# Vector work of the mixers moved from VectorE to GpSimd in a two-layer hybrid decoder

## The chip, the cores and the metric

The kernel runs on one core of one Trainium2 chip. The metric is device time in microseconds, the median of several runs. PE is TensorE, DVE VectorE, ACT ScalarE, Pool (POOL) GpSimd, and SP SyncE, which here issues nearly all DMAs. Each engine takes its instructions in the order of the program, and waits at the head of its queue where an instruction's inputs are not there yet.

## What is computed

Two layers over 1024 tokens of width 1024, all in float32. A layer is, from the reference:

```python
h = rms_norm(x, g_pre_mix)
z = h @ w_in
...
mix = jnp.concatenate([out_m, out_s.astype(x.dtype), out_d], axis=-1) @ w_out
x = x + rms_norm(mix, g_post_mix)
h2 = rms_norm(x, g_pre_mlp)
u = jnp.square(jax.nn.relu(h2 @ w_up))
x = x + rms_norm(u @ w_down, g_post_mlp)
```

The three mixers share the projection z: an mLSTM in chunks of 128 tokens (4 heads of 64), a causal sliding-window attention (window 128, 8 query heads on 2 key heads, sinks in the denominator), and a differential attention (4 heads, each with two maps of width 32, the second subtracted with a factor lambda). The queries and keys of the two attentions are rotated (rope): of the halves x1 and x2 of a head, x1 cos - x2 sin and x2 cos + x1 sin.

## The kernel before

**High and low parts.** Matmul operands are kept as a high part, rounded to the reduced float format that PE takes at full speed, and a low part, the rest. A product is three matmuls (high by high, high by low, low by high) into one PSUM bank. The helper `split` (L90) makes the parts: ACT casts the source into the high part (L91), DVE subtracts it from the source (L92). `load_split` (L94) does this for rows of the mixers' output (L98, L99), and `load_w` (L101) for weights: SP loads a piece of 512 columns into one of the two staging tiles of the pool "raw" (L107), then `split` follows. With a gain (the MLP's up weights) L114 and L115 take its place.

**Stages of a layer.** Normalised, transposed rows hT and lT (high and low) are multiplied by w_in in three ways. `proj_tiles` (L254) keeps weights stationary and gives columns of z transposed: queries and keys of the differential attention (`p_d`), those of the window attention (`p_s`), the mLSTM's (`p_m`). `g2` makes gates and values, `nat_group` the mLSTM's values and output gates. For the attentions the evacuation rotates: `rope_pair` (L301) has the first halves of the heads in one PSUM tile and the second halves in another. It makes four products from PSUM (L309, L310, L311, L313) and one difference and one sum in SBUF (L312, L314), and `hi_lo` (L293) then makes the high part (ACT, L296), stores it to a scratch matrix in DRAM, makes the low part (DVE, L298) and stores that.

The differential attention loads keys and queries back (L450 to L463) and goes in stages over steps of one head and 256 queries: scores on PE (L491), a masked minimum on DVE (L494), the exponential on ACT (L497), the subtraction of the second map on DVE (L504), transposes on PE (L518), their split (L91, L92) and the product with the values (L526). `diff3` normalises: ACT squares, DVE makes the mean, Pool takes the power -1/2 (L151) and multiplies (L543), DVE scales (L545). The window attention (`swa1`, `swa2`) has the same parts over steps of 128 queries and one key head (L601 to L639); it divides the exponentials by the denominator before the transposes, the first head of four on ACT (L618), the others on DVE (L620). The mLSTM goes over 8 chunks (`mlstm1` to `mlstm3`). All three store to the scratch matrix mix_d.

The out-projection (`out_group`, L811) takes mix_d in two groups of four k tiles. For each of 8 token tiles it loads mixed rows ("mxl", L97), makes their parts (L98 on ACT, L99 on DVE), multiplies them by w_out (L833) and copies or adds the result (L839, L841). The second group ends each token tile with `post_mix`: norm, residual (L977, L979) and the transposed input of the MLP.

**What sets the order.** The code is traced once. A scheduler then orders the instructions of every engine by priority, the place in the trace, by what their inputs allow and by its own estimate of how long things take. `ahead(n)` gives the priority of n instructions earlier: 1000 for weight loads and evacuations, 100000 for mixed rows and accumulations. `run` interleaves the streams of the mixers. A tile that is allotted again waits for the last reader of the buffer it replaces ("e" has 4 buffers, which mixed rows share with the attention's exponentials; "raw" has 2; "ev" has 6). So a change of one instruction's engine can move others, on all engines.

Of the kernel before, what the change touches and what calls it, by code (L numbers as in the profile page):

```python
# [10 lines left out]
F32 = mybir.dt.float32  # L11
# [3 lines left out]
ALU = mybir.AluOpType  # L15
# [13 lines left out]
# columns of the packed per-layer vector that every partition gets  # L29
# [5 lines left out]
def hybrid_kernel(ctx: ExitStack, tc: tile.TileContext, x_in, w_t, w_g, w_v, w_out, w_up, w_down,  # L35
# [15 lines left out]
    pool("big", 6)      # 16 KB  # L51
    pool("whl", 2)      # 8 KB: stationary weight tiles, high | low
    pool("wd", 4)       # 4 KB: operands of the differential attention, moving weights
    pool("ws", 4)       # 4 KB: operands of the window attention, moving weights
    pool("e", 4)        # 4 KB
    pool("at", 2)       # 4 KB
    pool("pt", 2)       # 4 KB
    pool("ev", 6)       # 2 KB
    pool("raw", 2)      # 2 KB
    pool("od", 3)       # 1 KB  # L60
    pool("ys", 1)       # 2 KB
# [24 lines left out]
    def ahead(n):  # L86
        """trace with the priority of n instructions earlier"""
        return tc.high_priority(offset=n) if n else nullcontext()

    def split(hi, lo, src):  # L90
        nc.scalar.copy(hi, src)  # L91
        nc.vector.tensor_sub(lo, src, hi.bitcast(F32))  # L92

    def load_split(hi, lo, src):  # L94
        """high and low parts of a matrix in DRAM; the low part's place takes the raw values first"""
# [3 lines left out]
        nc.vector.tensor_sub(lo, raw, hi.bitcast(F32))  # L99

    def load_w(hi, lo, src, step, gain=None):  # L101
        """high and low parts of a weight tile, through a staging tile, step columns at a time;
        gain has a factor for every P columns"""
        for c in range(0, hi.shape[1], step):
# [3 lines left out]
            with ahead(1000):  # L108
                if gain is None:
                    split(hi[:, c:c + step], lo[:, c:c + step], r)  # L110
                    continue
# [15 lines left out]
    # ---- constants  # L127
# [5 lines left out]
    tri_u = mk[:, P:2 * P]          # 1 where row <= col  # L133
    sel_l = mk[:, 2 * P:3 * P]      # row 127 all ones
    jj = mk[:, 3 * P:4 * P]         # [I64 0; I64 0]
    m_st = mk[:, 4 * P:5 * P]       # 0 where row <= col, else NEG
    # for negated scores: zeros | current block, previous block | current block
# [22 lines left out]
    def pre_norm_transpose(src, g, h, hT, lT, t):  # L160
        """h = rmsnorm(src) * g (without g: a factor of the weights that follow), transposed and split into hT/lT[:, t, kt, :]"""
# [1025 lines left out]
```

## Time and profile before

| | us |
|---|---|
| median of 3 runs | 2562.7 |
| lowest and highest run | 2557.64 and 2574.75 |
| span of the profiled execution | 2570.0 |
| mixers of layer 0 (from the start to the MLP's first full stretch) | 0 to 602 |
| MLP of layer 0, with PE full | 602 to 1250 |
| mixers of layer 1 | 1250 to 1872 |
| MLP of layer 1 | 1872 to 2570 |

The profile page has the time of the profiled execution only as its span, from the first to the last instruction on the core. Lines of the profile give the line of the kernel, the engine and the operation, the written tile and the read ones, the shape and the count, then busy time in us and the mean of one in ns, then the idle time of the engine before these instructions and what ended it. A row of waits reads: the waiting engine and line, what it waited for, us in total, times, the longest. In the timeline a row has start and duration in us, and in brackets the idle time before it. The chain of waits is followed back from the last instruction through what released each step. "SPq" is SP's queue of DMA issues. The granted clock of PE was 0.973 of full speed over the span.

### The profile page before, as it was taken

To read this page: it belongs to the slowest core of one execution; us is meant where nothing else is said; L and a number is where in the kernel's file an instruction comes from. 1 tells how busy PE (TensorE), PEld (TensorE's weight loads), DVE (VectorE), ACT (ScalarE), POOL (GpSimd) and SP (SyncE) were. 2 spreads that over 40 slices of the span, in tenths; PEclk is the share of its full clock that TensorE was granted. 3 is DMA by queue.
4 is the path that set the end of the run, shared out by engine and by line. 5 is a ranking of instruction groups with operands and counts; after the bars stand their busy time and mean duration, and the time that the engine had idled before them with its cause. 6 is when DMAs were issued, how large, how long until landed. Compare 5 with 4: busy or idle time off the path is not lost.

```text
span 2570.0 us, 32598 instructions
## 1 busy us (share of the span) xinstructions
PE 2395.5 (93%) x11556; PEld 1994.0 (78%) x11556; DVE 1449.0 (56%) x3540; ACT 1072.3 (42%) x2625; POOL 96.4 (4%) x174
## 2 busy tenths in 40 slices
PE   8988988789999999999999988887999999999998
PEld 7767866667888888888778867766788888888887
DVE  5676867676144334433684976876842344334436
ACT  4244766655323222321433745765653123213312
POOL 0000010011000000000010000100100000000000
PEclk9998989899999999999999998998999999999999
DMA  4444336353012111211543334554521122012104
GB/s 168 146 139 131 94 97 162 104 156 116 26 58 66 40 34 58 66 32 34 170 149 105 106 128 130 149 129 112 165 87 34 37 61 66 28 39 66 61 24 161
DMA packets 172115, 240.02 MB, mean 93 GB/s; under 512 B 24048, under 2 KB 86704, under 8 KB 171952
## 3 DMA queue, kind: packets, MB, share of 16 engines
q1 hardware_dynamic: 169792, 234.29, 29.9%
q10 hardware_dynamic: 2160, 3.65, 0.4%
q8 instruction: 91, 1.49, 0.3%
q14 instruction: 72, 0.59, 0.1%
HBM read 185.38 MB, written 52.49 MB: 93 GB/s over the span
## 4 chain that ended last, share of the span: by engine, by line
PE 72%; DMA 12%; DVE 7%; ACT 4%; issue 2%; POOL 1%; SPq 1%; POOLq 0%; DVEq 0%; ACTq 0%
PE pu L997 26%; PE pd L1042 25%; PE pt L283 7%; DMA mxl<-mix_d 3%; DMA qs<-d_rope 2%; PE pn L354 2%; PE pg L354 2%; PE po L833 2%; POOL rs L151 1%; PE sp L491 1%; PE pv L526 1%; DMA rw<-in_w_t_dram 1%; PE trd L518 1%; PE ss L601 1%; DMA mix_d<-ys 1%
## 5 line engine op out<-in xcount | busy, mean ns | idle before, releaser
L997 PE MATMUL pu<-h2T,wu 128*128 128x512 f32 x3072 | 700.3, 389 | 0.0
L997 PEld LDWEIGHTS pu<-h2T,wu 128*128 128x128 f32 x3072 | 576.3, 188 | 119.4
L1042 PE MATMUL pd<-wdh,u 128*128 128x512 f32 x2048 | 634.2, 389 | 1.3 <-DVE acm L1053 1.3
L1042 PEld LDWEIGHTS pd<-wdh,u 128*128 128x128 f32 x2048 | 384.2, 188 | 81.2 <-DVE acm L1053 1.8
L1042 PE MATMUL pd<-wdl,u 128*128 128x512 f32 x1024 | 398.6, 389 | 0.0
L1053 DVE TENSOR_TENSOR acm<-acm,pd 128x512 f32<-128x512 f32 x224 | 152.4, 686 | 303.1 <-PE pd L1042 303.1
L1000 ACT ACTIVATE r<-pu 128x512 f32<-128x512 f32 x128 | 75.3, 588 | 537.6 <-PE pu L997 537.4
L283 PE MATMUL pt<-hT,wt 128*128 128x512 f32 x832 | 287.8, 411 | 2.3 <-DVE lamp L226 1.5
L114 ACT ACTIVATE wu<-rw,gk 128x128 fp32r<-128x128 f32 x512 | 160.6, 390 | 186.7 <-PE pu L997 129.1
L115 DVE SCALAR_TENSOR_TENSOR wu<-rw,gk,wu 128x128 fp32r<-128x128 f32 x512 | 154.9, 351 | 131.9 <-ACT wu L114 131.2
L1042 PEld LDWEIGHTS pd<-wdl,u 128*128 128x128 f32 x1024 | 192.2, 188 | 39.8
L1003 DVE TENSOR_TENSOR r<-r 128x512 f32<-128x512 f32 x128 | 88.4, 691 | 226.2 <-ACT u L1002 226.2
L283 PEld LDWEIGHTS pt<-hT,wt 128*128 128x128 f32 x832 | 160.5, 196 | 33.4 <-issue 2.1
L151 POOL TENSOR_TENSOR rs<-ms,mhalf 128x1 f32<-128x1 f32 (+2 forms) x112 | 84.5, 758 | 2355.8 <-DVE ms L149 2287.2
L283 PE MATMUL pt<-lT,wt 128*128 128x512 f32 x416 | 170.5, 410 | 0.0
L92 DVE TENSOR_TENSOR wdl<-rw,wdh 128x512 fp32r<-128x512 f32 x128 | 88.6, 692 | 104.8 <-ACT wdh L91 104.8
L833 PE MATMUL po<-woh,mxl 128*128 128x512 f32 x384 | 133.9, 410 | 0.0
L91 ACT CAST wdh<-rw 128x512 fp32r<-128x512 f32 x128 | 79.3, 619 | 129.2 <-DMA rw<-in_w_down_dram 129.1
L497 ACT ACTIVATE e<-e,nb 128x256 f32<-128x256 f32 (+7 forms) x128 | 99.3, 777 | 50.9 <-DVE nb L494 47.0
L491 PE MATMUL sp<-ks,qs 96*128 96x512 f32 (+2 forms) x192 | 74.2, 397 | 40.3 <-DMA qs<-d_rope 27.6
L354 PE MATMUL pn<-wv,hT 128*128 128x256 f32 x512 | 110.6, 298 | 0.2 <-ACT mv L694 0.2
L283 PEld LDWEIGHTS pt<-lT,wt 128*128 128x128 f32 x416 | 82.1, 197 | 14.6 <-issue 0.4
(221 smaller groups left out, 3339.6 us busy)
## 6 DMA issues: line engine op xcount, KB each, us to landing
rw<-in_w_up_dram SPq DMA_DIRECT2D x128, 256.0 KB
rw<-in_w_down_dram SPq DMA_DIRECT2D x128, 256.0 KB
rw<-in_w_t_dram SPq DMA_DIRECT2D x52, 256.0 KB
tab<-in_rope_dram SPq DMA_DIRECT2D x20, 512.0 KB
xt<-in_x_dram SPq DMA_DIRECT2D x16, 512.0 KB
d_rope<-rot SPq DMA_DIRECT2D x32, 256.0 KB
s_ropeq<-rot SPq DMA_DIRECT2D x32, 256.0 KB
qq<-s_ropeq SPq DMA_DIRECT2D x16, 512.0 KB
```

Source lines behind the costliest of these rows:

```text
L92: nc.vector.tensor_sub(lo, src, hi.bitcast(F32))
L114: nc.scalar.activation(hi[:, cs], rj, AF.Copy, scale=g)
L115: nc.vector.scalar_tensor_tensor(out=lo[:, cs], in0=rj, scalar=g, in1=hi[:, cs].bitcast(F32), op0=ALU.mult, op1=ALU.subtract)
L151: nc.gpsimd.tensor_tensor(out=rs, in0=ms, in1=mhalf[:, 0:n], op=ALU.pow)
L283: nc.tensor.matmul(q, lhsT=a, rhs=b, start=n == 0, stop=n == 23)
L354: nc.tensor.matmul(q[:, 0:n], lhsT=a, rhs=b, start=i == 0, stop=i == 23)
L491: nc.tensor.matmul(sp[:, 0:w], lhsT=qs[0:96, m, (q % 4) * P:(q % 4 + 1) * P], rhs=ks[m][0:96, c0:c0 + w], start=True, stop=True)
L497: nc.scalar.activation(e[:, 0:L], e[:, 0:L], AF.Exp, bias=nb[:, nch - 1:nch], scale=-1.0, accum_out=den[:, m:m + 1])
L833: nc.tensor.matmul(q, lhsT=mx[:, a, k], rhs=wo[k][b][:, n * 512:(n + 1) * 512], start=i == 0, stop=i == 3 * nk - 1)
L997: nc.tensor.matmul(q, lhsT=w[:, a, kc], rhs=h2[b + half][:, :, kc], start=n == 0, stop=n == 23)
L1042: nc.tensor.matmul(q, lhsT=U[f][a][:, t * P:(t + 1) * P], rhs=D[f][b][:, n * 512:(n + 1) * 512], start=i == 0, stop=i == 3 * nf - 1)
L1053: nc.vector.tensor_add(a, a, q)
```

## The change

Work of DVE that reads and writes only SBUF goes to Pool, in the mixers alone: the low parts of weights without a gain in `proj_tiles`, `nat_group`, `out_group` and layer 1's gate weights; the low parts of mixed rows and of rotated rows; difference and sum of `rope_pair`; the normalisation of three of the four heads in the window attention; and three products or sums of the mLSTM. The low parts whose source is in PSUM, the MLP's weights and layer 0's gate weights stay on DVE. The second product that the rotation's sum takes gets a tile of its own, t2. Comments and docstrings go as well; they are left out here.

```diff
-    def split(hi, lo, src):
+    def split(hi, lo, src, eng=None):
         nc.scalar.copy(hi, src)
-        nc.vector.tensor_sub(lo, src, hi.bitcast(F32))
+        (eng or nc.vector).tensor_sub(lo, src, hi.bitcast(F32))
...
     def load_split(hi, lo, src):
         raw = lo.bitcast(F32)
         nc.sync.dma_start(raw, src)
         nc.scalar.copy(hi, raw)
-        nc.vector.tensor_sub(lo, raw, hi.bitcast(F32))
+        nc.gpsimd.tensor_sub(lo, raw, hi.bitcast(F32))
...
-    def load_w(hi, lo, src, step, gain=None):
+    def load_w(hi, lo, src, step, gain=None, eng=None):
...
-                    split(hi[:, c:c + step], lo[:, c:c + step], r)
+                    split(hi[:, c:c + step], lo[:, c:c + step], r, eng)
...
-                    load_w(hi, lo, w_t[l, i], 512)
+                    load_w(hi, lo, w_t[l, i], 512, eng=nc.gpsimd)
...
             store(0)
-            nc.vector.tensor_sub(r[:, 1], r[:, 1], r[:, 0])
+            nc.gpsimd.tensor_sub(r[:, 1], r[:, 1], r[:, 0])
             store(1)
...
-                nc.vector.tensor_sub(ra[:, 1], ra[:, 1], t)
-                nc.vector.tensor_mul(t, qb, c)
-                nc.vector.tensor_add(rb[:, 1], rb[:, 1], t)
+                nc.gpsimd.tensor_sub(ra[:, 1], ra[:, 1], t)
+                t2 = EV("t")
+                nc.vector.tensor_mul(t2, qb, c)
+                nc.gpsimd.tensor_add(rb[:, 1], rb[:, 1], t2)
...
-                    nc.vector.tensor_scalar(e[:, hh, 0:n], e[:, hh, 0:n], den[:, hh:hh + 1], None, ALU.mult)
+                    nc.gpsimd.tensor_scalar(e[:, hh, 0:n], e[:, hh, 0:n], den[:, hh:hh + 1], None, ALU.mult)
...
-                load_w(w[:, 0], w[:, 1], w_v[l, idx, :, 1024 * j:1024 * j + 1024], 512)
+                load_w(w[:, 0], w[:, 1], w_v[l, idx, :, 1024 * j:1024 * j + 1024], 512, eng=nc.gpsimd)
...
-                nc.vector.tensor_mul(ai, ai, qk[:, 0:2])
-            nc.vector.tensor_add(rb, rb, m_st.unsqueeze(1).broadcast_to([P, 4, P]))
+                nc.gpsimd.tensor_mul(ai, ai, qk[:, 0:2])
+            nc.gpsimd.tensor_add(rb, rb, m_st.unsqueeze(1).broadcast_to([P, 4, P]))
...
-            nc.vector.tensor_mul(hm[:, 0], hm[:, 0], sg.rearrange("p (h n) -> p h n", h=4))
+            nc.gpsimd.tensor_mul(hm[:, 0], hm[:, 0], sg.rearrange("p (h n) -> p h n", h=4))
...
-                load_w(hi, lo, w_out[l, kt * P:(kt + 1) * P, :], 512)
+                load_w(hi, lo, w_out[l, kt * P:(kt + 1) * P, :], 512, eng=nc.gpsimd)
...
-                    load_w(w[:, 0], w[:, 1], w_g[l, :, k, :], 392)
+                    load_w(w[:, 0], w[:, 1], w_g[l, :, k, :], 392, eng=nc.gpsimd)
```

The scheduler makes another order of it on every engine. Three places follow. In the changed kernel lines from `load_w` on are one or two higher than before (L99 is L98 of before, L313 is L312).

DVE at the first rotations of layer 0, where queries and keys of the differential attention leave PSUM ("pt" is the projection's PSUM tile, "tab" the cosines and sines). Before, for one pair of tiles:

```order
L309 TENSOR_TENSOR rot<-pt,tab 128x512
L310 TENSOR_TENSOR rot<-pt,tab 128x512
L311 TENSOR_TENSOR t<-pt,tab 128x512
L312 TENSOR_TENSOR rot<-rot,t 128x512
L313 TENSOR_TENSOR t<-pt,tab 128x512
L298 TENSOR_TENSOR rot<-rot 128x512
L314 TENSOR_TENSOR rot<-rot,t 128x512
L298 TENSOR_TENSOR rot<-rot 128x512
```

and now, the pair and what follows the last of them:

```order
L310 TENSOR_TENSOR rot<-pt,tab 128x512
L311 TENSOR_TENSOR rot<-pt,tab 128x512
L312 TENSOR_TENSOR t<-pt,tab 128x512
L315 TENSOR_TENSOR t<-pt,tab 128x512
L496 ISA e,nb<-sp,mdif 128x128
```

The difference, the sum and the two low parts have left DVE, and the attention's masked minimum (L496) stands four instructions nearer.

Pool a little later in layer 0, in the differential attention. Before, Pool has only the factors of the norms (rs):

```order
L151 TENSOR_TENSOR rs<-ms,mhalf 128x2
L543 TENSOR_TENSOR rs<-rs,rd 128x2
L151 TENSOR_TENSOR rs<-ms,mhalf 128x2
L543 TENSOR_TENSOR rs<-rs,rd 128x2
L151 TENSOR_TENSOR rs<-ms,mhalf 128x2
```

and now:

```order
L299 TENSOR_TENSOR rot<-rot 128x512 x3
L93 TENSOR_TENSOR wt<-rw,wt 128x512 x2
L299 TENSOR_TENSOR rot<-rot 128x512
L152 TENSOR_TENSOR rs<-ms,mhalf 128x2
L545 TENSOR_TENSOR rs<-rs,rd 128x2
L313 TENSOR_TENSOR rot<-rot,t 128x512
L299 TENSOR_TENSOR rot<-rot 128x512
L316 TENSOR_TENSOR rot<-rot,t 128x512
```

The factors now stand between sums and low parts of rotated rows and low parts of weights.

ACT in layer 0 where the out-projection's second group begins ("es" are the window attention's exponentials, "trs" its transposes, "ys" its outputs, "acc" the out-projection's results). Before:

```order
L610 ACTIVATE es,den_5033<-es,nb_5031 128x256
L98 CAST mxl<-mxl 128x512
L610 ACTIVATE es,den_5033<-es,nb_5031 128x256 x3
L613 ACTIVATE es_5032<-es_5032 128x4
L839 COPY acc_5198<-po 128x512
L618 ACTIVATE es<-es,den_4977 128x256
L618 ACTIVATE es<-es,den_5033 128x256
L638 COPY ys<-pvs 64x512
```

and now:

```order
L794 ACTIVATE mb_3892<-mb_3892 128x256
L806 COPY mb_3892<-tbm 128x256
L841 COPY acc_5206<-po 128x512
L99 CAST mxl<-mxl 128x512
L841 COPY acc_5206<-po 128x512
L99 CAST mxl<-mxl 128x512
L841 COPY acc_5206<-po 128x512 x2
L99 CAST mxl<-mxl 128x512
```

The casts of mixed rows for that group now come after the last instructions of the window attention and of the mLSTM (tbm is its last transpose), close behind one another.

## The prediction

> **What bounds the kernel now.** I read the page first, then stage windows, then each engine's waits.
>
> ```profile
> span 2570.0 us, 32598 instructions
> PE 2395.5 (93%) x11556; PEld 1994.0 (78%) x11556; DVE 1449.0 (56%) x3540; ACT 1072.3 (42%) x2625; POOL 96.4 (4%) x174
> DVE  5676867676144334433684976876842344334436
> PE 72%; DMA 12%; DVE 7%; ACT 4%; issue 2%; POOL 1%; SPq 1%; POOLq 0%; DVEq 0%; ACTq 0%
> ```
>
> Pool has next to nothing to do, but the chain that ended last holds only 7% of DVE; DMA holds 12%. The high digits of DVE are the two mixers (0 to 602 us and 1250 to 1872 us). Between them the MLP keeps PE full and the change does not touch it. So the 1224 us of the mixers are all there is to win from. By stage (span; PE, PEld, DVE, ACT, POOL busy; clock; DMA):
>
> ```profile
> 96.00:256.00 160.00, 130.49 (x693) 109.13 (x692) 107.45 (x287) 67.47 (x173) 7.43 (x14) 0.89 0.44 135
> 384.00:546.00 162.00, 131.29 (x668) 106.06 (x667) 114.05 (x386) 101.18 (x287) 6.04 (x6) 0.91 0.50 135
> 1472.00:1600.00 128.00, 107.48 (x600) 91.51 (x599) 87.34 (x234) 57.99 (x153) 7.00 (x14) 0.91 0.42 129
> 1640.00:1810.00 170.00, 133.10 (x725) 109.73 (x724) 119.28 (x406) 104.21 (x306) 9.46 (x12) 0.91 0.51 134
> sum 1224.00, PE 1057.10 PEld 886.03 DVE 879.34 ACT 671.82 POOL 91.14; mean PE 96.10 PEld 80.55 DVE 79.94 ACT 61.07 POOL 8.29
> ```
>
> PE is idle 167 us of the 1224. DVE is at 67 to 70% in these four stages: a crowd that delays others, not the bound by itself. In the window and mLSTM stage of layer 0 (384 to 546 us) the waits say who holds whom:
>
> ```profile
> ACT mxl L98 <- DMA mxl<-mix_d: 31.5, 11, 8.2
> DVE mxl L99 <- ACT mxl L98: 22.8, 9, 6.5
> ```
>
> ACT stands 31.5 us before casts of mixed rows that their DMA has not landed, and DVE stands 22.8 us behind ACT. So this stage is held by an in-order engine waiting for a load. A faster DVE does not shorten that; another place of the cast in ACT's order does.
>
> **The change, part by part.** The sum starts from the profiled execution's span, 2570.0 us; the page shows no time around it, and the median of the runs, 2562.7, is 7.3 us lower, inside their spread of 2557.64 to 2574.75. What leaves DVE, in its large groups:
>
> ```profile
> L92 DVE TENSOR_TENSOR wt<-rw,wt 128x512 fp32r<-128x512 f32 x52 | 35.0, 685 | 30.9 <-ACT wt L91 30.6
> L298 DVE TENSOR_TENSOR rot<-rot 128x512 f32<-128x512 f32 x36 | 24.7, 686 | 3.5 <-ACT rot L296 3.5
> L620 DVE TENSOR_SCALAR es<-es,den 128x256 f32<-128x256 f32 x84 | 25.0, 345 | 0.0
> L99 DVE TENSOR_TENSOR mxl<-mxl 128x512 fp32r<-128x512 f32 x32 | 22.1, 689 | 49.9 <-ACT mxl L98 49.5
> L92 DVE TENSOR_TENSOR wol<-rw,woh 128x512 fp32r<-128x512 f32 x24 | 16.2, 689 | 6.1 <-ACT woh L91 5.3 <-PE ss L601 0.2
> L312 DVE TENSOR_TENSOR rot<-rot,t 128x512 f32<-128x512 f32 x16 | 11.0, 686 | 0.1
> L314 DVE TENSOR_TENSOR rot<-rot,t 128x512 f32<-128x512 f32 x16 | 11.0, 685 | 0.0
> ```
>
> These are 145 us; the smaller ones (low parts of wv, wo and wg, three mLSTM products, the 128-wide normalisations) bring it to about 190, in all some 216 two-input instructions of 512 columns, 30 of 256, 8 of 392, and 96 one-input ones.
>
> The price on Pool is not in this trace; the nearest rows are:
>
> ```profile
> L543 POOL TENSOR_TENSOR rs<-rs,rd 128x2 f32<-128x2 f32 x32 | 7.3, 228 | 2.4
> L722 POOL MEMSET mb<- 128x130 f32 x4 | 0.8, 201 | 0.0
> L718 POOL MEMSET mb<- 128x260 f32 x2 | 0.6, 315 | 8.1 <-PE pt L283 8.1
> ```
>
> A multiply of two columns costs 0.228 us, nearly all fixed. The two memsets differ by 130 columns and 114 ns: 0.88 ns a column for one stream. If all streams of a two-input instruction overlap, 512 columns cost 0.228 + 512 x 0.88 = 0.68 us; if two reads and the write go one after another, 0.228 + 1536 x 0.88 = 1.58. I take the middle, two streams, 1.13 us, against 0.69 on DVE; a normalisation 0.45 against 0.345. Pool then gets about 216 x 1.13 + 30 x 0.68 + 8 x 0.92 + 96 x 0.44 = 314 us, and with the 91 it has, 405 of 1224, a third; at 1.58 it is 43%. So Pool doesn't become the bound by volume. (The Trainium skill, "GPSIMD Engine Reference", section "Elementwise — side-by-side cycle accounting", gives a two-input add 1.96 times DVE's time and advises against such moves; an estimate by that ratio is 1.35 us, 48 us more on Pool, and the same sum.)
>
> Term 1, the order. The new order puts the casts of the second out-projection group behind the last window attention and mLSTM instructions of ACT, where before they stood among them. What ACT waited at these casts, in the larger cases (four of layer 0, one of layer 1):
>
> ```profile
> 480.52 0.62 ACT L98 CAST mxl<-mxl 128x512 fp32r<-128x512 f32 x1 [1.69 <-DMA mxl<-mix_d]
> 500.75 0.62 ACT L98 CAST mxl<-mxl 128x512 fp32r<-128x512 f32 x1 [4.76 <-DMA mxl<-mix_d]
> 532.96 0.62 ACT L98 CAST mxl<-mxl 128x512 fp32r<-128x512 f32 x1 [8.16 <-DMA mxl<-mix_d]
> 554.03 0.62 ACT L98 CAST mxl<-mxl 128x512 fp32r<-128x512 f32 x1 [1.79 <-DMA mxl<-mix_d]
> 1766.15 0.62 ACT L98 CAST mxl<-mxl 128x512 fp32r<-128x512 f32 x1 [5.76 <-DMA mxl<-mix_d]
> ```
>
> These rows hold 22 us, the smaller waits between them 3: minus 25. The casts of the first group stay close behind the copies whose store they read, or now stand right behind the out-projection that frees their tile; I leave their waits as they are. Bounds: 0 (the stall only moves) to -62.4, all waits of L98.
>
> Term 2, moved work on the chain. The chain of the mixers passes 54 pieces of moved DVE work, 31.5 us, the first and last:
>
> ```profile
> 86.66 0.69 DVE wt L92
> 1850.70 0.69 DVE mxl L99
> ```
>
> Where the next step needs the result, it returns on Pool at 1.13/0.69; where it only stood in DVE's queue, it goes. I take two thirds needed: 21 x 1.64 - 31.5 = +3. Bounds: -31.5 (none needed) to +41 (all needed, at 1.58).
>
> Term 3, DVE's head of queue. In 96 to 256 us:
>
> ```profile
> DVE wt L92 <- ACT wt L91: 10.9, 2, 6.6
> ACT e L497 <- DVE nb L494: 22.9, 16, 6.6
> ```
>
> DVE stood behind ACT's cast of a weight, and ACT's exponential behind DVE. That head of queue is now Pool's. I take the longest, -7; bounds 0 to -11.
>
> Term 4, Pool's queue. The factors rs now stand in order behind subtractions. In post-mix, where rs is on the chain, 16 tiles meet a mixed row's low part half of the time: 16 x 0.5 x 1.13 = 9, half of it covered by the other tiles' matmuls: +5. Without that cover, and for both rs of a tile, +36. In the attention DVE waits for rs (L543) already, by the list of who waited for it (us, times):
>
> ```profile
>   DVE on L545: 13.9, 20
> ```
>
> It will wait longer, under DVE's own spare time; I cost it at nothing.
>
> Term 5, staging. Two tiles hold raw weights, and SP's load of the next piece waits for the low part:
>
> ```profile
> SPq L107 <- DVE wt L92: 36.3, 25, 6.2
> ```
>
> Each of these 25 waits grows by 0.44 us, 11 us of SP; behind it stand the stores of rotated rows and the loads of queries. Weights are loaded far ahead of use, so I take a fifth: +2.
>
> Term 6, contention. Pool already waits beside DVE:
>
> ```profile
> 350.36 0.69 POOL L151 TENSOR_TENSOR rs<-ms,mhalf 128x2 f32<-128x2 f32 x1
> 375.38 1.18 POOL L151 TENSOR_TENSOR rs<-ms,mhalf 128x2 f32<-128x2 f32 x1 [23.11 <-DVE ms L149]
> 375.25 0.75 DVE L670 SCALAR_TENSOR_TENSOR yc<-z,cvt,yc 128x512 f32<-128x512 f32 x1
> ```
>
> The same power operation takes 0.69 alone and 1.18 when it begins under a DVE instruction that reads two SBUF tensors. L670 alone runs 35.8 us:
>
> ```profile
> L670 DVE SCALAR_TENSOR_TENSOR yc<-z,cvt,yc 128x512 f32<-128x512 f32 x48 | 35.8, 746 | 2.6 <-ACT yc L664 2.1 <-issue 0.2
> ```
>
> With the attention's and post-mix's instructions of this kind I estimate four times that, a tenth of the 1224 us: each of Pool's 350 moved instructions then waits some 0.05 us, 17 us of Pool time, of which I put +2 on the path. The normalisation of the windows, three in a row, takes 1.35 instead of 1.03 us a step; only 4.6 us of PE waits are put to L620 in all 32 steps, so this is covered: 0, and uncovered 32 x 0.3 to 32 x 1.0.
>
> The sum: -25 + 3 - 7 + 5 + 2 + 2 = -20, so a span of 2550, and 7.3 lower for the median: **2543 us**.
>
> **Rivals.** (B) More gain: the freed DVE lets the differential attention follow PE. PE is idle 29.5 and 20.5 us in the stages from 96 and from 1472; if half of that closes (-25) and half of the other 37.6 us before L98 as well (-19), it ends at 2499. For it: DVE now has four instead of eight instructions for a pair of rotated tiles ahead of the attention's scans. Against: the longest pieces of the chain there are loads of queries:
>
> ```profile
> 127.39 11.85 DMA qs<-d_rope
> 1473.18 11.16 DMA qs<-d_rope
> ```
>
> (C) No change: DVE was off the path and the stall before L98 only moves to another load: 2563.
>
> (D) Slower: staging decides. A weight tile of two pieces serves 48 matmuls, at 0.227 us (43.52 us for 192 in the MLP's chain) 10.9 us of PE. Load 6.4 (below), cast 0.62 and low part 1.13 leave 2.7 us. As soon as Pool's queue in front of a low part is over 2.7 us (three rotation instructions), PE, ACT or SP waits for weights. If each of the 108 pieces then ends 0.44 us later on the path: +48, 2591. For it: SP's waits above, and the rotations, which come in fours on Pool. Against: the loads' small share of the chain now.
>
> ```profile
> 99.92 6.43 DMA rw<-in_w_t_dram
> 772.26 43.52 PE pu L997 x192
> ```
>
> (E) DVE locked out. If a running Pool instruction also stops DVE, 64 + 48 + 32 instructions with two SBUF inputs (L504, L670, post-mix) each find Pool busy a third of the time and wait half of 1.13 us: 27 us, on the path 2570. Here DVE instructions that began under Pool kept their time, but Pool then read only a few columns. The Trainium skill, "SBUF — State Buffer", section "Who interferes with whom", states such an exclusive lock in both directions; the Pool rows above agree with one, no run here shows the other.
>
> That the change does not move the work is excluded by the order: Pool's rows grow from 99 to 335.
>
> **How the numbers follow.** Forecast 40%, with its own range of 2515 to 2565; B 22%, C 10%, D 22%, E 6%. A measurement can tell about 1%, 25.6 us: faster below 2537, slower above 2588. Of the forecast 18 points lie below 2537; with B, 40% faster. The other 22 with C and E make 38%; D 22% slower. The range of 2490 to 2592 leaves out the far half of B and of D; unknown costs (terms 1 and 2) span about as much.
>
> **What would show it.** Right: Pool near 400 us busy and DVE near 1260; a 512-column Pool instruction between 0.68 and 1.58 us; ACT's wait before the cast of mixed rows near 37 us instead of 62; Pool, not DVE, standing behind weight casts. Wrong: that wait unchanged (C); PE or ACT waiting for Pool's low parts, or longer SP waits at L107 with PE idle (D); two-input DVE instructions longer than now (E); PE's idle time in the differential stages halved (B).

## The result, and the profile after

| | before | after |
|---|---|---|
| median, us | 2563.95 | 2682.65 |
| lowest and highest run | 2557.64 and 2574.75 | 2680.68 and 2689.47 |
| span of the profiled execution | 2570.0 | 2682.3 |

The ratio is 1.0462, with a 95% interval of 1.0441 to 1.0483: 119 us slower, where 2543 us was forecast and the range ended at 2592. The top of the page of after:

```profile
span 2682.3 us, 32761 instructions
PE 2431.1 (91%) x11556; PEld 2012.2 (75%) x11556; DVE 1345.7 (50%) x3190; ACT 1075.9 (40%) x2625; POOL 489.7 (18%) x524
...
PE   7878987679999999999988978876899999999998
...
DVE  5356865526344344433573875655462443344436
```

No engine's share of the span grew except Pool's, and Pool is at 18%. Of the 112 us by which the profiled span grew, 77 are more idle time of PE and 36 a longer busy time for the same 11556 matmuls; PE's granted clock over the span went from 0.973 to 0.961, and how much of the 36 that makes was not separated. All the loss is in the mixers; the MLPs take as long as before. The mixers of layer 0 lose 54 us and those of layer 1 57 us, counted from the layer's start to the last out-projection matmul (po, 593 us before, 647 after, in layer 0). Layer 1's start is taken at one place near the end of layer 0's MLP, 1203 us in the kernel before.

To see where, cut each mixer at its own events. Layer 0 before, from 96 us on: to the differential attention's last scores (sp); to the last projection matmul (pt); to the last transpose of the mLSTM (tbm); to the last po. The columns are the span and the busy time of PE, PEld, DVE, ACT and Pool with counts, then PE's granted clock and DMA:

```profile
96.00:341.00 245.00, 214.56 (x1236) 182.49 (x1235) 181.98 (x511) 133.50 (x349) 14.30 (x30) 0.93 0.39 119
341.00:383.00 42.00, 29.49 (x142) 23.46 (x141) 24.92 (x68) 23.25 (x64) 5.48 (x16) 0.87 0.35 102
383.00:563.00 180.00, 147.63 (x744) 118.82 (x743) 129.80 (x428) 108.73 (x307) 9.43 (x11) 0.92 0.49 136
563.00:593.00 30.00, 26.43 (x134) 20.95 (x133) 24.06 (x39) 22.55 (x38) 6.63 (x10) 1.00 0.55 178
```

and after, cut at the same events:

```profile
96.00:335.00 239.00, 197.49 (x1133) 166.85 (x1132) 150.35 (x444) 118.18 (x321) 72.47 (x74) 0.91 0.38 113
335.00:425.00 90.00, 74.07 (x358) 58.24 (x356) 58.98 (x151) 61.20 (x165) 40.68 (x49) 0.93 0.36 108
425.00:575.00 150.00, 105.33 (x487) 82.76 (x487) 72.37 (x232) 70.28 (x199) 69.60 (x71) 0.81 0.45 117
575.00:647.00 72.00, 64.04 (x299) 51.04 (x298) 40.56 (x71) 42.69 (x80) 24.31 (x26) 1.00 0.47 152
```

Read the counts. Beside the differential attention PE does 1133 matmuls instead of 1236, and the attention is only 6 us shorter for it. So 90 us instead of 42 are needed until the projections are through. Then PE is busy for 70% of the window and mLSTM stage instead of 82%, at a clock of 0.81 instead of 0.92, and 72 us of out-projection come behind it instead of 30. PE's work is the same; it stands at other places of PE's queue.

What the prediction looked at did happen. The wait in front of the casts of mixed rows, over the whole run, before and after:

```profile
ACT mxl L98 <- DMA mxl<-mix_d: 62.4, 21, 8.2
ACT mxl L99 <- DMA mxl<-mix_d: 36.4, 15, 6.4
```

It was 62.4 us, and 37 were forecast. The time did not follow it.

What Pool took for the moved work, by form:

```profile
L622 POOL TENSOR_SCALAR es<-es,den 128x256 f32<-128x256 f32 x84 | 78.4, 948 | 44.8 <-DVE den L617 36.1 <-ACT sb L92 5.4 <-ACT ys L640 3.0
L93 POOL TENSOR_TENSOR wt<-rw,wt 128x512 fp32r<-128x512 f32 x52 | 69.5, 1352 | 776.2 <-ACT wt L92 776.2
L299 POOL TENSOR_TENSOR rot<-rot 128x512 f32<-128x512 f32 x36 | 48.1, 1349 | 27.8 <-ACT rot L297 27.8
L100 POOL TENSOR_TENSOR mxl<-mxl 128x512 fp32r<-128x512 f32 x32 | 42.5, 1327 | 48.7 <-ACT mxl L99 48.6
```

A two-input instruction of 512 columns takes 1.33 to 1.35 us in these rows and 1.27 to 1.41 over all groups, inside the bounds of 0.68 to 1.58. The normalisation takes 0.95 us, not 0.45. And Pool now waits at its head for what it never waited for (384 to 610 us, who waited for whom: us, times, longest):

```profile
POOL mb L746 <- DMA mb<-m_rows: 45.4, 8, 7.5
ACT mb L748 <- POOL mb L746: 21.0, 4, 7.2
...
PE tbm L804 <- POOL mb L798: 16.5, 4, 8.1
```

The mLSTM's mask sum (L746, L744 before) stands before a late load, and low parts, normalisations and the gate product (L798) stand behind it. Before, DVE did this sum, and in the same stretch it waited little for the load:

```profile
DVE mb L744 <- DMA mb<-m_rows: 4.6, 1, 4.6
```

So there were three theories. **Order**: the scheduler wrote another order for every queue, and that costs. **Head of Pool's queue**: L746 blocks Pool. **Price**: the longer instructions lie on the path.

### The profile page after: what moved, and what is told of

Its sections match the earlier page's. It is cut to its first block, busy times and chain, and to the rows that moved or that the text cites. A ratio compares the mean times of both kernels' runs of the same rounds, so it can differ in the third digit from the quotient of the medians.

```text
span 2682.3 us, 32761 instructions
## 1 busy us (share of the span) xinstructions
PE 2431.1 (91%) x11556; PEld 2012.2 (75%) x11556; DVE 1345.7 (50%) x3190; ACT 1075.9 (40%) x2625; POOL 489.7 (18%) x524
## 5 line engine op out<-in xcount | busy, mean ns | idle before, releaser
L152 POOL TENSOR_TENSOR rs<-ms,mhalf 128x1 f32<-128x1 f32 (+2 forms) x112 | 78.6, 703 | 1035.1 <-DVE ms L150 1020.8
L93 POOL TENSOR_TENSOR wt<-rw,wt 128x512 fp32r<-128x512 f32 x52 | 69.5, 1352 | 776.2 <-ACT wt L92 776.2
```

The costliest lines, as they stand in the source:

```text
L93: (eng or nc.vector).tensor_sub(lo, src, hi.bitcast(F32))
```

## The experiments

All kernels are the changed one with two additions. Switches say which of five groups go to Pool: weights, rotation, norm, mixed, mlstm. And a queue can be held to the order of another variant, its plan, by edges that fix only the order of issue:

```diff
-                    nc.gpsimd.tensor_scalar(e[:, hh, 0:n], e[:, hh, 0:n], den[:, hh:hh + 1], None, ALU.mult)
+                    (nc.gpsimd if "norm" in ON else nc.vector).tensor_scalar(e[:, hh, 0:n], e[:, hh, 0:n], den[:, hh:hh + 1], None, ALU.mult)
...
+                for k in order:
+                    ins = traced[k]
...
+                        tc.add_manual_dep(ins, row[-gap].name, mybir.DependencyInfo(
+                            mybir.DependencyClass.NoSync, mybir.DependencyReason.DATA), reason="order")
```

Here `order` is the plan's final order. PINS names the queues that are held; the others are ordered anew. GAP is how strictly DVE is held: 1 is the exact order, 2 the order to within three places (it was 2 for all five groups and for the rotation in the old order). Instructions that have changed engine are held only among each other; where they stand among the rest of their new queue, the scheduler chose. Each diff below shows only the switches, with the engines' names shortened.

**1. Engine or order?** All on Pool, the old order on the queues of PE, SP, ACT and DVE:

```diff
+ON = ("weights", "rotation", "norm", "mixed", "mlstm")
+PLAN, PINS, GAP = (), ("PE", "SP", "Activation", "DVE"), 2
```

> The changed kernel's operations, all 350 moved ones on Pool, but PE, SP and ACT run their instructions in exactly the order of the kernel before, and DVE the ones it keeps in that order too, to within three places; the moved ones keep on Pool the order that they had among each other on DVE. It tells the new order from the new engine. Theory 'order' (the loss of 119 us comes from the order that the scheduler wrote for the new engines: projections and out-projections later, less filler in the window and mLSTM stage): about the time before, 2550 to 2585 us. Theory 'engine' (it comes from what the moved instructions cost and wait for on Pool, whatever the order): near the time of the change, 2640 to 2700 us. In between, 2590 to 2640, both have a share.

Measured 2609.4 us, ratio 1.0169 (1.0151 to 1.0188). The converse, nothing on Pool, the new order on all queues:

```diff
+ON = ()
+PLAN, PINS, GAP = ("weights", "rotation", "norm", "mixed", "mlstm"), ("PE", "SP", "Activation", "DVE", "Pool"), 1
```

> The converse: none of the 350 instructions is moved (all on DVE), but PE, SP, ACT and the rest of DVE and Pool keep exactly the order of the changed kernel; the instructions that are back on DVE keep the order that they had among each other on Pool. Theory 'order': near the time of the change, 2660 to 2690 us, since the late projections and the tail of out-projection matmuls after the window and mLSTM stage are in this order. Theory 'engine': near the time before, 2555 to 2600 us.

Measured 2660.5 us, 1.0375 (1.0355 to 1.0394). The new order alone costs 96 us with none of the 350 instructions on Pool; Pool alone, in the old order, costs 44. The two add to 140 where the change lost 119, so they overlap: with all on Pool, the step from the old order to the new is 75 us. The converse came out as "order" had it, the first run between the two theories. Layer 0 of the second kernel at the same events:

```profile
96.00:328.00 232.00, 193.28 (x1127) 161.87 (x1126) 170.67 (x492) 119.00 (x320) 12.62 (x27) 0.93 0.38 116
328.00:410.00 82.00, 69.83 (x356) 54.33 (x354) 63.05 (x184) 60.89 (x165) 5.38 (x18) 0.99 0.40 118
410.00:558.00 148.00, 99.33 (x486) 79.70 (x486) 89.56 (x293) 69.67 (x197) 9.42 (x8) 0.85 0.44 117
558.00:631.00 73.00, 65.88 (x299) 52.35 (x298) 47.61 (x83) 42.98 (x81) 8.53 (x14) 0.98 0.45 150
```

The stretches of after were 90, 150 and 72 us; here they are 82, 148 and 73, with Pool nearly idle. The loss has the shape of the order, not of Pool.

**2. Head of Pool's queue, and the price of the normalisation**, both in the new order on all queues:

```diff
+ON = ("weights", "rotation", "norm", "mixed")
```

> The changed kernel in its own order, with the three mLSTM instructions (the product of L745, the mask sum of L746, the gate product of L798; 46 in all) back on DVE. The mask sum waits for a late load (45.4 and 40.5 us of Pool's idle time in the two mixers) and the normalisation, the low parts and the gate product stand behind it on Pool. Theory 'head of Pool's queue': this wait gone from Pool, TensorE's waits for the gate product (16.5 + 13.1 us) and SP's (19.3 us in the first mixer) shrink with it: 2610 to 2645 us. Theory 'order' and theory 'price of the normalisation': 2665 to 2685 us.

Measured 2680.4 us, 1.0446 (1.0430 to 1.0461): nothing came back. The same stage of this kernel:

```profile
POOL es L622 <- DVE den L617: 28.7, 8, 10.6
DVE mb L746 <- DMA mb<-m_rows: 23.5, 7, 6.2
...
PE tbm L804 <- DVE mb L783: 12.2, 3, 6.6
PE tbm L804 <- DVE mb L798: 8.5, 3, 5.5
```

The wait for the load moved to DVE, where the same sum waited 4.6 us in the old order, and PE waits there. So the wait comes with the new order, whichever engine has the sum; it was a symptom. That theory fell.

```diff
+ON = ("weights", "rotation", "mixed", "mlstm")
```

> The changed kernel in its own order, with the window attention's normalisation (L622, 98 instructions of 128 x 256 or 128 x 128, three to a step) back on DVE. Theory 'price of the normalisation': on Pool one of 256 columns takes 0.95 us where DVE took 0.35, a step 2.73 us instead of 1.03; 32 steps are 55 us of a chain that TensorE's weighted sums wait for, of which half to all comes back: 2625 to 2660 us. Theory 'order' and theory 'head of Pool's queue': 2670 to 2685 us.

Measured 2671.9 us, 1.0421 (1.0401 to 1.0442): 11 us back, a tenth of the loss and half of the least that the price theory gave.

**3. One group at a time, in the old order** (PLAN = (), the same four queues held), to share out the 44 us:

```diff
+ON = ("weights",)
```

> Only the low parts of the mixers' weights are on Pool (108 instructions: wt, wg, wv, wo, wol), and PE, SP, ACT and the rest of DVE keep exactly the order of the kernel before. The five groups together cost 44 us in that order; this run and the next two share that out. Theory 'price on the chain' (a moved instruction costs its longer time, 1.30 against 0.69 us for 512 columns, where something waits for it at once): a weight tile is used long after it is split, so nothing waits for its low part: 2555 to 2572 us, the time before. Theory 'Pool and DVE hinder each other' (the cost goes with Pool's busy time, whatever it works on): these are 140 of the 394 us that Pool gained, so a third of the 44: 2575 to 2585 us.

```diff
+ON = ("rotation",)
```

> Only the rotation (the difference L313, the sum L316, the low part L299: 68 instructions, with the second t tile) is on Pool, in the order of the kernel before (DVE to within three places). Theory 'price on the chain': each pair of rows passes a difference or sum and a low part, 2 x 0.61 us longer, and waits behind one another on Pool, ahead of the stores from which the differential attention's operands come, for which TensorE waits; some eight pairs a mixer lie in the stretch where it waits: 2575 to 2590 us. Theory 'hinder each other': 88 of Pool's 394 us: 2570 to 2577 us. Nothing, if the stores have slack: 2560 to 2570 us.

```diff
+ON = ("norm",)
```

> Only the window attention's normalisation (L622, 98 instructions) is on Pool, in exactly the order of the kernel before. Theory 'price on the chain': a step is 2.7 us on Pool where it was 1.0 on DVE, for 32 steps 55 us, of which TensorE's fillers hide half to two thirds: 2580 to 2595 us. Theory 'hinder each other': 87 of Pool's 394 us: 2570 to 2577 us. Nothing, if the fillers hide all: 2560 to 2570 us.

```diff
+ON = ("mixed",)
```

> Only the mixed rows' low parts (32 instructions) are on Pool, in exactly the order of the kernel before. Of the 44 us that the five groups cost in that order the weights made 15, the normalisation 8 and the rotation -4. Theory 'price on the chain': the low part is the last thing that an out-projection group of TensorE needs, 0.61 us longer each, on Pool at once instead of behind DVE's other work: 2560 to 2572 us. If the rest of the 44 us is these rows': 2580 to 2590 us.

```diff
+ON = ("mlstm",)
```

> Only the three mLSTM instructions (46 in all) are on Pool, in exactly the order of the kernel before. Theory 'price on the chain': a block of the mLSTM passes all three, 0.6 + 0.4 + 0.4 us longer, 16 blocks in all, 22 us, of which fillers hide a half or more; Pool is free, so nothing stands behind the mask sum that waits for its load: 2562 to 2576 us. If the rest of the 44 us is here: 2580 to 2590 us; if neither these nor the mixed rows cost it, it comes from several groups sharing Pool's queue.

| on Pool | time, us | ratio (interval) |
|---|---|---|
| weights | 2583.4 | 1.0059 (1.0036 to 1.0082) |
| rotation | 2566.9 | 0.9985 (0.9965 to 1.0004) |
| norm | 2575.1 | 1.0030 (1.0017 to 1.0043) |
| mixed | 2567.2 | 1.0001 (0.9988 to 1.0014) |
| mlstm | 2571.6 | 1.0027 (1.0012 to 1.0042) |

The price theory missed the weights, the rotation and the normalisation, and held for the mixed rows and the mLSTM. "Hinder each other" had the weights and the normalisation and missed the rotation, which has as much of Pool's time as the normalisation and costs nothing. The dearest group is the one whose results nobody waits for at once: the price theory had it at nothing. Two things show in its trace. SP's loads wait for Pool's low parts (first 620 us, where before they waited 9.3, 7.7 and 5.4 us for DVE's):

```profile
SPq L108 <- POOL wt L93: 43.2, 15, 21.5
...
SPq L108 <- POOL wv L93: 14.9, 6, 6.2
...
SPq L108 <- POOL wol L93: 13.2, 10, 3.1
```

And DVE's own instructions get longer; three groups in this kernel:

```profile
L608 DVE CUSTOM_DVE_ANT_0 es<-ss,m_swa 128x256 f32<-128x256 f32 x112 | 43.7, 417 | 13.4 <-PE ss L603 12.7 <-PE trs L632 0.3
L672 DVE SCALAR_TENSOR_TENSOR yc<-z,cvt,yc 128x512 f32<-128x512 f32 x48 | 42.8, 892 | 4.8 <-ACT yc L666 3.9 <-issue 0.2
...
L504 DVE SCALAR_TENSOR_TENSOR r<-den,nlam,rd 128x1 f32<-128x1 f32 x64 | 18.0, 281 | 0.7
```

and the first and the last of them before (the middle one, L670 there, took 746 ns):

```profile
L606 DVE CUSTOM_DVE_ANT_0 es<-ss,m_swa 128x256 f32<-128x256 f32 x112 | 43.9, 418 | 12.5 <-PE ss L601 11.5 <-PE trs L630 0.3
...
L502 DVE SCALAR_TENSOR_TENSOR r<-den,nlam,rd 128x1 f32<-128x1 f32 x64 | 13.6, 212 | 0.6
```

DVE instructions that read two SBUF tensors lengthen (746 to 892 ns, 212 to 281); one that reads PSUM keeps its time (418 and 417). Over all groups that are the same in both kernels this is 44 us more on DVE with the weights on Pool, 15 with the rotation, 2 with the normalisation, 54 in the changed kernel. Longer DVE instructions alone do not set the time: the rotation has 15 us of them and costs nothing, the normalisation 2 and costs 8. Which of the two, SP's waits or DVE's longer instructions, makes the 15 us of the weights was not separated. The five singles add to 1.02%, all together cost 1.69%; the other 17 us appear only with all five on Pool.

**4. Which part of the order?** TensorE's alone, with nothing on Pool:

```diff
+ON = ()
+PLAN, PINS = ("weights", "rotation", "norm", "mixed", "mlstm"), ("PE",)
```

> None of the 350 instructions is moved; TensorE alone is held to exactly the order of the changed kernel, all other queues are ordered anew by the scheduler for this. With all queues in the changed kernel's order it was 2660.5 us. Theory 'filler' (the loss lies in TensorE's own order: 25 us of out-projection matmuls between the steps of the window attention and the mLSTM of the first mixer where there were 51, and the rest behind them as a tail): 2640 to 2665 us again. Theory 'other queues' (ACT's, DVE's or SP's order makes the steps late, and TensorE's order would do no harm): 2565 to 2600 us.

Measured 2697.8 us, 1.0498 (1.0478 to 1.0517), more than with all queues in the new order (2660.5) and above the ranges of both theories. I read this as "filler": out-projection matmuls that no longer stand between the steps of window attention and mLSTM. Two runs were to prove it. First, the old order of the last stretch of PE's queue put back, all on Pool:

```diff
+    plan = engines, mix(order, build(())[1][1])
```

where `mix` sorts the last 707 and 748 TensorE instructions of the two mixers by their old places.

> The changed kernel, all 350 on Pool, TensorE in its new order except for the last stretch of each mixer: the 707 and 748 TensorE instructions behind the last projection (window attention, mLSTM, out-projection, the transposes behind it) stand among each other as in the kernel before; the other queues are ordered anew by the scheduler for this. In the changed kernel 131 and 138 of 384 out-projection matmuls stand ahead of the mixer's last mLSTM transpose, in the kernel before 289 and 309. Theory 'filler': what that stretch lost comes back, some 20 to 30 us a mixer: 2620 to 2645 us. Theory 'late projections' (the loss is made ahead of the stretch, where projections end 41 and 93 us later): 2670 to 2685 us. Below 2615 us the stretch would be the whole of what the order costs.

Measured 2700.7 us, 1.0529 (1.0512 to 1.0547): slower, not 40 to 60 us faster, and above the 2685 of the other theory too. With the matmuls back among the steps, the stage from the last projection to the last mLSTM transpose went from 150 to 193 us:

```profile
422.00:615.00 193.00, 135.31 (x641) 108.51 (x639) 89.47 (x264) 87.35 (x235) 82.93 (x82) 0.84 0.42 112
615.00:647.00 32.00, 28.60 (x136) 22.95 (x137) 24.33 (x37) 23.39 (x38) 9.39 (x13) 0.95 0.56 181
```

The matmuls only changed sides; this mixer ended at 647 us, as in the changed kernel, and what was lost besides came in layer 1. Second, one small group with an order of its own:

```diff
+ON = ("norm",)
```

> Again only the window attention's normalisation on Pool, but now the scheduler writes the order for it. It puts 174 and 176 of 384 out-projection matmuls ahead of the mixers' last mLSTM transpose (289 and 309 in the kernel before, 131 and 138 in the changed one); the projections stay about where they were. In the order before it took 2575 us. Theory 'filler': some 120 matmuls a mixer of 0.23 us go from between the steps to the tail, 27 us a mixer, of which a half to all is lost: 2600 to 2630 us. Theory 'the order does not matter for one small group': 2570 to 2585 us.

Measured 2574.5 us, 1.0039 (1.0026 to 1.0053): the order took 120 filler matmuls a mixer out and cost nothing that can be told against the old one (1.0030). "Filler" fell twice.

What was left is ahead of that stage: the late projections. The mirror run, old order in the first part of PE's queue, new in the last, all on Pool:

```diff
-            for n, k in zip(run, sorted((order[n] for n in run), key=at.get)):
+            for n, k in zip(seg, sorted((order[n] for n in seg), key=at.get)):
                 order[n] = k
```

Here `run` are the places of the last stretch and `seg` those ahead of it.

> The mirror of the run with the old order in the last stretch: all 350 on Pool, and TensorE in its new order except for the first part of each mixer: the 1873 and 1800 TensorE instructions up to the last projection (gates, projections, differential attention, the first steps of the window attention) stand among each other as in the kernel before, and the last stretch stays new (131 and 138 of 384 out-projection matmuls ahead of the last mLSTM transpose). So 77 and 46 projection matmuls stand behind the differential attention's last scores, not 191 and 182. Theory 'late projections' (the mixer ends some 205 to 225 us after its last projection whatever stands in between, and the new order puts that projection 41 and 53 us later): 2590 to 2630 us. If the first part's order is no cause either, and the loss lies in how the two parts go together: 2660 to 2690 us.

Measured 2717.8 us, 1.0585 (1.0568 to 1.0603). That fell too, as a matter of PE's queue alone. Then groups with the scheduler's own orders, chosen by how far they shift the projections:

```diff
+ON = ("norm", "mixed", "mlstm")
```

> Normalisation, mixed rows' low parts and the mLSTM's three on Pool (176 instructions), weights and rotation on DVE as before, the order the scheduler's own for this. It leaves the projections where they were (79 and 47 matmuls behind the differential attention's last scores, 77 and 46 in the kernel before) and takes as many out-projection matmuls out of the window and mLSTM stage as the whole change did (147 and 149 ahead of the last mLSTM transpose; 131 and 138 there, 289 and 309 before). Theory 'late projections': the sum of the three singles in the old order, 8 + 0 + 7 us: 2572 to 2592 us. If the out-projection matmuls did matter: 2610 to 2640 us.

```diff
+ON = ("rotation", "weights")
```

> The other half: weights and rotation on Pool, the rest on DVE, the order the scheduler's own for this. It puts the projections where the whole change put them (192 and 182 matmuls behind the differential attention's last scores) and keeps somewhat more out-projection matmuls in the last stage (168 and 192). In the old order the two singles cost 15 and -4 us. Theory 'late projections': these, and 60 to 96 us of order: 2635 to 2675 us. If several groups sharing Pool's queue were the cause: 2575 to 2600 us.

```diff
+ON = ("rotation",)
```

> Only the rotation on Pool (68 instructions), which in the old order cost nothing (ratio 0.9985), now in the order that the scheduler writes for it: 140 and 121 projection matmuls stand behind the differential attention's last scores, about half way from the kernel before (77 and 46) to the changed one (191 and 182). Theory 'late projections': about half of what the order costs (96 us with all on DVE): 2600 to 2625 us. If only the full shift matters, or none: 2560 to 2580 us.

| on Pool | projection matmuls behind the last scores, layers 0 and 1 | ratio in the scheduler's own order (interval) | in the old order | order's share, us | first part of the two mixers against before, us |
|---|---|---|---|---|---|
| norm | 79, 47 | 1.0039 (1.0026 to 1.0053) | 1.0030 | 2 | +1 |
| norm, mixed, mlstm | 79, 47 | 1.0117 (1.0102 to 1.0132) | 1.0058 (sum) | 15 | +10 |
| rotation | 140, 121 | 1.0110 (1.0095 to 1.0125) | 0.9985 | 32 | +37 |
| rotation, weights | 192, 182 | 1.0276 (1.0259 to 1.0293) | 1.0044 (sum) | 60 | +79 |
| all five | 191, 182 | 1.0462 (1.0441 to 1.0483) | 1.0169 | 75 | +94 |
| none, held to the order of all five | 191, 182 | 1.0375 (1.0355 to 1.0394) | 1 | 96 | +87 |

Before has 77 and 46. The order's share is the difference of the two ratios times 2565 us; in the rows with a sum it also holds what the groups cost by sharing Pool, since the sum leaves that out. The last column is the time from the layer's start to its last projection matmul, both layers, against 383 + 443 us before. Where all queues have one order made together, the share rises with the shift of the projections, and most of the loss is made in the first part. That is a correlation and no proof: the row of three groups has 15 us with the projections in place, and putting them back on PE's queue alone made the kernel slower. In the first part the changed kernel loses 94 us; from the last projection to the last out-projection matmul the changed kernel loses only 12 and 5 us (222 and 222 against 210 and 217). The run with three groups lay above its 2572 to 2592, and the rotation's just under its range.

**5. One queue alone, all on Pool:**

```diff
+PLAN, PINS = (), ("SP",)
```

> All 350 on Pool; SP alone (the queue that issues nearly all loads and stores) is held to exactly the order of the kernel before, and the scheduler writes the order of TensorE, ACT, DVE and Pool anew for this. With no more than that TensorE's order comes out near the old one: 92 and 62 projection matmuls behind the differential attention's last scores (77 and 46 before, 191 and 182 in the changed kernel), 286 and 294 of 384 out-projection matmuls ahead of the last mLSTM transpose (289 and 309; 131 and 138). With all queues in the old order it was 2609.4 us. Theory 'the schedule as a whole' (late projections and late out-projection together, set by the order of loads and stores): 2595 to 2630 us. If it needs ACT's and DVE's old order too: 2650 to 2690 us.

Measured 2685.3 us, 1.0463 (1.0434 to 1.0491), with PE's order near the old one all the same, as the second theory had it.

```diff
+PLAN, PINS = (), ("PE",)
```

> All 350 on Pool; TensorE alone is held to exactly the order of the kernel before, and the scheduler writes the other queues' orders anew for this (SP's among them). Half of TensorE's old order with half of its new one gave 2700.7 and 2717.8 us. Theory 'the schedule as a whole, TensorE's two parts together': 2600 to 2635 us, as with all queues in the old order. If the other queues' new orders are what made the halves slow: 2660 us or more.

Measured 2662.4 us, 1.0368 (1.0342 to 1.0395), again as the second theory had it. Layer 0 of this last kernel, whose PE queue is that of before to the last instruction:

```profile
96.00:366.00 270.00, 224.16 (x1246) 186.76 (x1245) 173.26 (x468) 135.93 (x356) 83.67 (x83) 0.92 0.36 110
366.00:407.00 41.00, 30.16 (x144) 23.79 (x143) 22.26 (x50) 24.40 (x66) 16.19 (x26) 0.86 0.39 103
407.00:610.00 203.00, 153.34 (x738) 124.28 (x736) 110.00 (x338) 107.26 (x298) 98.05 (x96) 0.87 0.45 120
```

The counts are those of before (1236, 142, 744), the stretches are 270, 41 and 203 us instead of 245, 42 and 180. With ACT, DVE and SP in the old order as well, the mixer ended at 606 instead of 641 us. So the old order works as a set as far as these runs go: one queue's old order with the others' orders made anew gives back 20 us or nothing, four queues' together 75.

What stays open: which pair of queues must agree, and why the scheduler's order for less DVE work is worse on the chip. No run held ACT and DVE to the old order without PE and SP. No version beat the kernel before; the rotation alone in the old order came nearest (0.9985, an interval that holds 1).

## Why the prediction was wrong, point by point

- **Term 1, the order (-25, bounds 0 to -62.4): this is the step that failed.** The wait it counted did go (62.4 to 36.4 us). But the new order was costed by one wait on one queue, and its bounds had no plus side. With none of the moved work on Pool it costs 96 us, and 75 with all of it there. The reading under the term, that ACT's wait for the load holds the window and mLSTM stage, failed with it: the wait fell, and PE's busy share in that stage fell too, from 82% to 70%. The same order that took ACT's waits away put some 100 matmuls fewer beside the differential attention. Which wait it lengthens instead stays open.
- **Terms 2 to 6 together (+5):** Pool's share, measured in the old order, was +44, of which the five singles make 26. This is the second miss, and about a third of the first.
- **Term 2, moved work on the chain (+3, bounds -31.5 to +41):** no run measured it apart from the other terms. The 1.13 us were 1.33 to 1.35, and the normalisation's 0.45 were 0.95 (0.97 with the other four groups off Pool, so their company is not the reason). Uncovered, the normalisation was bounded at 32 us; a step of three now takes 2.7 us instead of 1.0, and yet the group alone costs 8 us: the cover I named holds for most of it.
- **Term 3, DVE's queue (-7):** it did not come. With the weights alone on Pool, DVE's wait for ACT's cast of a weight is gone in the stretch from 96 to 256 us, and yet ACT waits 21.5 us there for the attention's minimum instead of 22.9; in the changed kernel it waits 28.4.
- **Term 4, Pool's queue (+5, +36 uncovered):** the wait I had not seen, the mask sum before its load, is larger than the one I costed (45.4 us in layer 0 alone), and taking it off Pool gave nothing.
- **Term 5, staging (+2) and rival D (2591, 28 above the time before):** weights alone cost 15 us. SP's waits for the low parts of wt grew from 36.3 to 101.3 us there, by 65 where the term counted 11. The sign was D's; the part of staging, and that of the contention beside it, are not separated. D was the only rival clearly on the slower side and held about an eighth of the loss.
- **Term 6, contention (+2), and rival E:** DVE's two-input instructions lengthen as E said, and DVE's in all by 54 us where E counted 27. What of it reaches the path was not measured. "DVE near 1260" became 1345.7 for that reason in part.
- **B and C:** PE's idle time beside the differential attention did not halve; PE's share there went from 88% (214.56 of 245) to 83%. C had the stall only moving; it shrank, and the time grew.

The missing rival was: the order that the scheduler makes for the moved work is itself worse. A sign of it was at hand in the two orders, on PE: 77 and 46 projection matmuls behind the last scores before, 191 and 182 after; it shows how far the order has moved, not what that costs. I read ACT's, DVE's and Pool's rows, not those of the engine that is 93% busy.

## What to carry to other kernels

When a scheduler orders the queues, moving work between engines is two changes: look at the new order first, on the bound engine, count what stands beside each stage that waits, and let the cost of the order have both signs. The counts say that the order has moved, not its price: here PE's old queue among newly ordered ones was still 3.7% slower than before, where the old order on four queues was 1.7%. To tell the two apart, run the new engines in the old order and the old engines in the new one, holding all queues; a single queue held while the others move shows little. A wait that is the largest in a list may be a symptom: here one shrank from 62.4 to 36.4 us and one left its engine, and the time did not follow.

## What the runs showed of the hardware that was not expected

Pool's two-input instruction of 512 columns takes 1.35 us against 0.69 on DVE, 1.97 times (low parts of wt, 1352 and 685 ns). The Trainium skill, "GPSIMD Engine Reference", section "Elementwise — side-by-side cycle accounting", gives 1.96; the trace agrees. A one-input multiply by a factor for each partition is dearer still by that measure: 0.948 us for 256 columns against 0.345, 2.75 times. And the slowing goes both ways. The prediction showed it on Pool, where the same power operation took 0.69 and 1.18 us; here DVE's instruction on two SBUF tensors went from 746 to 898 ns on average (L672 in the changed kernel), while L608, which reads PSUM, kept 418 ns. The Trainium skill, "SBUF — State Buffer", section "Who interferes with whom", says that a DVE instruction with two SBUF inputs contends with a Pool instruction that reads SBUF, and that one with at most one SBUF input does not, unless it is in a mode that uses both ports. The first two rows below agree. The last two, before and after, are of an instruction with one input, and it lengthened too, from 167 to 272 ns; whether it runs in such a mode, no row shows.

```profile
L672 DVE SCALAR_TENSOR_TENSOR yc<-z,cvt,yc 128x512 f32<-128x512 f32 x48 | 43.1, 898 | 9.9 <-ACT yc L666 9.6
L608 DVE CUSTOM_DVE_ANT_0 es<-ss,m_swa 128x256 f32<-128x256 f32 x112 | 44.5, 418 | 31.5 <-PE ss L603 22.8 <-ACT es L615 7.7 <-PE trs L632 0.5
L149 DVE TENSOR_SCALAR ms<-ss 128x2 f32<-128x2 f32 x32 | 5.3, 167 | 13.8 <-ACT on L540 13.5
L150 DVE TENSOR_SCALAR ms<-ss 128x2 f32<-128x2 f32 x32 | 8.7, 272 | 13.7 <-ACT on L542 13.5
```
